# Attention values by halves of the queries, with the masked correction cut to 64 keys and its high and low part stacked

## The chip, the cores and the metric

The kernel runs on one core of one Trainium2 chip. The metric is the device time of one execution in microseconds (us). Five engines work side by side, each through its own instructions in the order in which they are written: TensorE (PE; PEld is its weight loading), VectorE (DVE), ScalarE (ACT), GpSimd (POOL) and SyncE (SP), which issues most of the DMA transfers. POOL and ACT issue some transfers too.

## The reference, cut to what matters

One residual block of a decoder, sequence 1024, width 1024, in float32. The part that is changed is sliding-window attention: 16 heads of 64, in four groups that share keys and values, blocks of 128 queries, a window of 128 keys, and one learned sink per head.

```
s = jnp.einsum('bnqkgd,bnskd->bnkgqs', qb, kb) * (1.0 / math.sqrt(hd))
diff = qi + BLOCK - kj
band = (diff >= 0) & (diff < WINDOW)
...
p = jnp.exp(s - m)
denom = jnp.sum(p, axis=-1, keepdims=True) + jnp.exp(sink - m)
o = jnp.einsum('bnkgqs,bnskd->bnqkgd', p / denom, vb)
```

A query q of a block (0 to 127) sees the keys 0 to q of its own block and the keys q+1 to 127 of the block before: for each key position exactly one of the two blocks. So there are 128 weights for a query, and the output is the sum over k of p[k] times v of the previous block, plus, where k is at most q, p[k] times the difference of the two v. The other parts of the block (input projection, rotary embedding, a gated linear recurrence, gates, the output projections, two norms) are unchanged. The first block of a sequence has no previous one.

## The kernel before

Matmuls work on float32 numbers that are split into a high and a low part, and the large projections use a scheme with seven half-size products for eight. Everything runs in an order that is written out by hand (`manual_schedule` for all five engines): instructions reach each engine in program order. In the input projection, a slot holds one product of twelve 128x512 matmuls, and `background` places further groups of ACT and DVE steps by planned costs; `slots(d)` waits d slots.

**Preparation of v.** `v_prep(g)` runs for each of the four groups g of heads in that background: `f0` loads v of the group, `f1` takes the difference d of neighbouring blocks (for the first block v itself), `f2` writes the high parts of v and d into the tiles `vs` and `dv` (columns 0 to 63), `f3` the low parts (columns 64 to 127), and stores both tiles to `vs_d[g]` and `dv_d[g]` from SP, 512 KB each. The tiles have one buffer each, so `f2` of the next group writes over what those stores read.

**Attention.** There are 32 units u: group u // 8, block n = u % 8. Four heads are handled at once, so a unit's weights are a tile of 128 keys x (4 heads x 128 queries). One pass of the loop is called a step here and works on several units, in this program order:

- `scores(u)`: eight matmuls into `s_ps`; `maxima_a` (ACT copy of the current block's scores to `p`), `maxima_d` (DVE lays the previous block's scores over them where the key is past the query, L1297; for n = 0 POOL fills with -1e30 instead, L1300; then the maximum, L1302). The units of one pair share a load of keys and queries (`load_kq`, SP).
- `weights_a(u-1)`: four exponentials on ACT (L1307).
- `piece()`: twelve matmuls of the recurrent branch's output projection (L174; the last products of the input projection, L696, in the first steps), whose weights ACT casts (L104) and DVE splits (L110).
- `weights_d(u-1)`: reciprocal and normalization on DVE (L1313, L1314).
- `values(u-3)`: the products of this case (L1355) into `pv`. Then `join_a` (ACT, L1364 and L1365) and `join_d` (DVE, L1375 and L1376) add the high and low halves of the output rows.
- `transposed(u-2)`: four transposes into `pt` (L1321); `split_a` casts the high part `phc` (ACT, L1326), `split_d` subtracts the low part `plc` (DVE, L1332).
- POOL: `sink(u+1)` copies the sinks (L1271); `masks(u-2)` makes `phm` and `plm`, copies of `phc` and `plc` with zeros where the key is past the query (L1341).
- DVE and ACT: the output gate of a finished pair (`a_prep`: L1491, L1496, L1501), one of its steps in each pass, and `do_later`: L104 and L110 for the coming pieces.

`values` multiplies the full pieces by `vs` of the previous block and the masked pieces by `dv`: four matmuls with 512 columns. For n = 0 there are two, with `dv`. `load_v(m)` brings `vs` and `dv` of a pair of units from HBM through POOL's queue, two transfers, and stands inside `values` of the even units. `phc`, `plc`, `phm`, `plm`, `pt`, `pv` and `s_ps` have one buffer each.

Of the kernel before, what the change touches and what calls it, by code (L numbers as in the profile page):

```python
# [12 lines left out]
F32 = mybir.dt.float32  # L13
F32R = mybir.dt.float32r
# [4 lines left out]
ALU = mybir.AluOpType  # L19
# [3 lines left out]
P = 128  # L23
# [5 lines left out]
NG = 4  # L29
# [23 lines left out]
def tile_hybrid_block(ctx, tc, x, x_t, pk, rows, posr, posi, c_row, w_ss, w_gate, w_main, w_v,  # L53
                      w_g, w_ap, w_rp, w_out, out):
    nc = tc.nc
    V, A, G, T = nc.vector, nc.scalar, nc.gpsimd, nc.tensor

    def dma(dst, src, eng=nc.sync):
        dst, src = (a.bitcast(F32) if a.dtype == F32R else a for a in (dst, src))
        return eng.dma_start(dst, src)  # L60

    def f32(ap):
        return ap.bitcast(F32)
# [65 lines left out]
    vs_d = [tc.dram_tile([P, 8, P], F32, name=f"vs_d{g}") for g in range(NG)]  # L129
    dv_d = [tc.dram_tile([P, 8, P], F32, name=f"dv_d{g}") for g in range(NG)]  # L130
# [440 lines left out]
    def make_operands(i):  # L571
        for t in (i, i + 4):
# [8 lines left out]
    W = {}  # L581
# [11 lines left out]
                    channel_multiplier=-1)  # L593
# [47 lines left out]
    class Load:  # L641

        pe = act = dve = 0.0
# [555 lines left out]
    def v_prep(g):  # L1199
        t = {}  # L1200
        vpp = W["vpp"]

        def f0():
            t["v"] = vpp.tile([P, 8, 64], F32, tag="v32", name="v32")
            dma(t["v"][:], v_d[:, :, g, :])

        def f1():
            t["d"] = vpp.tile([P, 8, 64], F32, tag="d32", name="d32")
            V.tensor_tensor(out=t["d"][:, 1:8, :], in0=t["v"][:, 1:8, :],
                            in1=t["v"][:, 0:7, :], op=ALU.subtract)  # L1210
            V.tensor_copy(t["d"][:, 0, :], t["v"][:, 0, :])

        def f2():
            for n_ in ("vs", "dv"):
                t[n_] = vpp.tile([P, 8, P], F32R, tag=n_, name=n_)
            A.copy(t["vs"][:, :, 0:64], t["v"][:])
            A.copy(t["dv"][:, :, 0:64], t["d"][:])

        def f3():
            for n_, d_, dst in (("v", "vs", vs_d), ("d", "dv", dv_d)):  # L1220
                V.tensor_tensor(out=t[d_][:, :, 64:128], in0=t[n_][:],
                                in1=f32(t[d_][:, :, 0:64]), op=ALU.subtract)
# [8 lines left out]
    at = psx = None  # L1231
    U = {}
# [22 lines left out]
        dma(qs[:], q_d[g].rearrange("(a j) t -> a j t", j=4)[:, :, t0:t0 + 256])  # L1255
        U["kq", m] = ks, qs

    def load_v(m):
        g, n0 = m // 4, (m % 4) * 2
        vs = at.tile([P, 2, P], F32R, tag="vs", name="vs", bufs=2)  # L1260
        dv = at.tile([P, 2, P], F32R, tag="dv", name="dv", bufs=2)
        dma(dv[:], dv_d[g][:, n0:n0 + 2, :], G)
        lo = 0 if n0 else 1
        dma(vs[:, lo:, :], vs_d[g][:, n0 - 1 + lo:n0 + 1, :], G)
        U["v", m] = vs, dv

    def sink(u):
        px = at.tile([P, 4, P + 1], F32, tag="p", name="p", bufs=3)
# [64 lines left out]
        U["m", u] = phc, plc  # L1333

    def masks(u):
        phc, plc = U["m", u]
        ms = []
        if u % 8:
            for s_, tag in ((phc, "phm"), (plc, "plm")):
                d_ = at.tile([P, 4, P], F32R, tag=tag, name=tag)  # L1340
                G.affine_select(out=d_[:], in_=f32(s_[:]), pattern=[[0, 4], [1, P]],  # L1341
                                compare_op=ALU.is_ge, fill=0.0, base=0,
                                channel_multiplier=-1)
                ms.append(d_)
        U["m", u] = [phc, plc], ms

    def values(u):
        n = u % 8
        vs, dv = U["v", u // 2]
        full, masked = U.pop(("m", u))  # L1350
        prods = [((vs if n else dv)[:, n % 2, :], m) for m in full]
        prods += [(dv[:, n % 2, :], m) for m in masked]
        pv = psx.tile([P, 4 * P], F32, tag="v", name="pv")
        for i, (b, m) in enumerate(prods):
            W["pe"] = T.matmul(pv[:], b, m[:].rearrange("p j q -> p (j q)"),  # L1355
                               start=(i == 0), stop=(i == len(prods) - 1))
        U["pv", u] = [pv[:].rearrange("p (a e q) -> p a e q", a=2, e=2)]
# [280 lines left out]
    for u in range(32 + 3):  # L1638
# [178 lines left out]
    for c in range(2, KC):  # L1817
# [21 lines left out]
        if c > 5:  # L1839
            n = 0 if c == 6 else 3  # L1840
# [84 lines left out]
    for n in range(24):  # L1925
        p, kc = n // 4, n % 4
# [67 lines left out]
    for i in range(3):  # L1994
        f = fs[i]
# [8 lines left out]
    f = small()  # L2004
# [91 lines left out]
```

## Time and profile before

| | |
|---|---|
| median of 3 runs | 912.93 us (912.89 to 913.12) |
| profiled execution, span from first to last instruction | 910.2 us |
| the runs' median less that span (start and end around it) | 2.7 us |
| PE busy | 892.0 us, 98% of the span |
| DVE busy | 722.1 us, 79% |
| ACT busy | 557.6 us, 61% |
| POOL busy | 125.2 us, 14% |
| moved by DMA | 182.05 MB, 200 GB/s over the span |
| attention, first scores to last values | 563 to 735 us |

The page gives no own time for the profiled execution beside its span; the runs' times are those of whole executions. A line of the timeline has the start in us from the span's start, the duration in us, the engine, the line of the kernel, the operation, the tiles as written<-read, shapes, and in brackets the engine's idle time before it and who ended it. The groups give count, busy time, mean duration in ns and idle time before. Matmuls are pipelined, so their recorded durations overlap.

### The profile page before, as it was taken

What the parts mean: (1) busy time and instruction counts of PE and PEld (TensorE: products, weight loads), DVE (VectorE), ACT (ScalarE), POOL (GpSimd) and SP (SyncE); (2) the same over time, 40 slices, a digit from 0 to 9 for tenths busy, and PEclk for the clock granted to TensorE, in tenths of its full rate; (3) what the DMA queues carried; (4) which work ended last, traced back from release to release, by engine and by line L of the source; (5) the groups of instructions that cost most, each with busy time, mean ns of one, the idle gap of its engine ahead of it and who ended that gap; (6) DMA issues with size and microseconds to landing.
All of it is one profiled execution on the core that took longest, in us unless ns stands there. A gap on an engine that the chain in (4) does not pass through costs nothing.

```text
span 910.2 us, 12609 instructions
## 1 busy us (share of the span) xinstructions
PE 892.0 (98%) x4187; PEld 740.7 (81%) x4187; DVE 722.1 (79%) x1143; ACT 557.6 (61%) x1088; POOL 125.2 (14%) x204
## 2 busy tenths in 40 slices
PE   5999999999999999999999999999999999999997
PEld 3879888887888788888887888888888888888886
DVE  7976889797679983988498576899999946779875
ACT  6753655454566755775678685888888731114555
POOL 0120000000010010000000001354444421310002
PEclk9999999999999999999999999999999999999998
DMA  9963458862344362346155257996666259878314
GB/s 351 414 212 110 163 168 312 281 230 85 116 144 151 116 234 86 115 151 225 36 197 166 84 192 253 338 368 215 203 199 219 93 172 330 306 273 322 140 46 185
DMA packets 88598, 182.05 MB, mean 200 GB/s; under 512 B 13891, under 2 KB 30275, under 8 KB 88534
## 3 DMA queue, kind: packets, MB, share of 16 engines
q1 hardware_dynamic: 81908, 161.57, 51.0%
q0 software_dynamic: 6336, 19.37, 5.9%
q8 instruction: 33, 0.54, 0.2%
q14 instruction: 31, 0.25, 0.1%
q10 hardware_dynamic: 290, 0.32, 0.1%
HBM read 124.49 MB, written 57.12 MB: 200 GB/s over the span
## 4 chain that ended last, share of the span: by engine, by line
PE 87%; DVE 5%; DMA 4%; ACT 2%; issue 1%; POOL 0%; SPq 0%; DVEq 0%; ACTq 0%
PE bk L696 43%; PE rp L174 13%; PE bo L1869 7%; PE pmain L174 6%; PE pgate L991 5%; PE bk L174 3%; PE s_ps L1283 3%; PE pv L1355 2%; DMA r<-w_main 2%; PE pt L1321 1%; DVE wl L110 1%; PE bk L1529 1%; PE bk L1528 1%; PE bk L1527 1%; DMA wada<-w_ss 1%
## 5 line engine op out<-in xcount | busy, mean ns | idle before, releaser
L696 PE MATMUL bk<-nh,wl 128*128 128x512 f32 x352 | 137.4, 390 | 0.4 <-DVE wl L110 0.4
L696 PE MATMUL bk<-nh,wh 128*128 128x512 f32 x352 | 137.1, 389 | 0.0
L696 PE MATMUL bk<-nl,wh 128*128 128x512 f32 x352 | 137.0, 389 | 0.0
L110 DVE TENSOR_TENSOR wl<-r,wh 128x512 fp32r<-128x512 f32 x113 | 80.5, 727 | 7.4 <-ACT wh L104 7.4
L104 ACT CAST wh<-r 128x512 fp32r<-128x512 f32 x113 | 68.6, 618 | 21.6 <-PE bk L1529 12.2
L60 POOL DMA_DIRECT2D wq_d<-wq x32 | 22.0, 687 | 423.7 <-DVE wq L1181 379.3
L696 PEld LDWEIGHTS bk<-nh,wl 128*128 128x128 f32 x352 | 66.1, 188 | 15.1 <-DVE wl L110 1.5
L696 PEld LDWEIGHTS bk<-nh,wh 128*128 128x128 f32 x352 | 66.1, 188 | 13.8
L696 PEld LDWEIGHTS bk<-nl,wh 128*128 128x128 f32 x352 | 66.1, 188 | 13.6
L696 PE MATMUL bk<-hh,wl 128*128 128x512 f32 x176 | 68.6, 390 | 0.4 <-DVE wl L110 0.4
L696 PE MATMUL bk<-hh,wh 128*128 128x512 f32 x176 | 68.6, 390 | 0.0
L696 PE MATMUL bk<-hl,wh 128*128 128x512 f32 x176 | 68.5, 389 | 0.0
L110 DVE TENSOR_TENSOR wl<-ws,wh 128x512 fp32r<-128x512 f32 x76 | 51.7, 683 | 0.0
L1307 ACT ACTIVATE p<-p,small 128x129 f32<-128x129 f32 x128 | 50.1, 401 | 0.0
L104 ACT CAST wh<-ws 128x512 fp32r<-128x512 f32 x76 | 45.8, 614 | 0.1
L1869 PE MATMUL bo<-wh,sum 128*128 128x512 f32 x128 | 39.6, 389 | 0.0
L696 PEld LDWEIGHTS bk<-hh,wh 128*128 128x128 f32 x176 | 33.0, 188 | 7.7 <-ACT wh L104 0.9
L696 PEld LDWEIGHTS bk<-hh,wl 128*128 128x128 f32 x176 | 33.0, 188 | 7.5 <-DVE wl L110 0.8
L696 PEld LDWEIGHTS bk<-hl,wh 128*128 128x128 f32 x176 | 33.0, 188 | 6.9
L1283 PE MATMUL s_ps<-ks,qs 128*128 128x256 f32 (+1 forms) x256 | 37.6, 289 | 0.2 <-DVE p L1297 0.2
L799 ACT ACTIVATE c<-bk 128x512 f32<-128x512 f32 x29 | 17.3, 597 | 30.2 <-PE bk L696 30.2
L696 PE MATMUL bk<-hha,wl 128*128 128x512 f32 x88 | 34.5, 392 | 0.6 <-DVE wl L110 0.5
(412 smaller groups left out, 2336.7 us busy)
## 6 DMA issues: line engine op xcount, KB each, us to landing
r<-w_main SPq DMA_DIRECT2D x100, 256.0 KB, 4.3
wada<-w_ss SPq DMA_DIRECT2D x16, 512.5 KB, 9.0
qs<-q_d SPq DMA_DIRECT2D x16, 512.0 KB, 5.8
wq_d<-wq POOLq DMA_DIRECT2D x24, 256.0 KB, 4.6
wr<-wq_d SPq DMA_DIRECT2D x24, 256.0 KB, 5.0
ks<-k_d SPq DMA_DIRECT2D x24, 192.0 KB, 5.0
wq<-w_out POOLq DMA_DIRECT2D x16, 256.0 KB, 5.7
q_d<-rhi SPq DMA_DIRECT2D x16, 256.0 KB, 4.1
```

Of the source, the lines that this page charges most:

```text
L60: return eng.dma_start(dst, src)
L104: A.copy(dst[0][:], src)
L110: V.tensor_tensor(out=dst[1][:], in0=src, in1=f32(dst[0][:]), op=ALU.subtract)
L174: mm = T.matmul(ps[hf], ww, xx[kc][hf], start=(kc == 0 and ww is w_h and xx is xh), stop=(kc == KC - 1 and xx is xl))
L696: W["pe"] = T.matmul(ps, ww[:, c], b[kc][xx_], start=(first and kc == 0 and i == 0), stop=(kc == 3 and i == 2), skip_group_check=not first)
L799: A.activation(t["t"], s(), AF.Tanh, scale=0.5)
L991: W["pe"] = T.matmul(ps[:, SL[hf]], ww[:, c0:c0 + P], xx_[:, SL[hf]], start=(ic == 0 and i == 0), stop=(ic == 1 and i == 2))
L1283: W["pe"] = T.matmul(o, qs[:, j, qc], ks[:, b, k0 + (0 if n else P):k0 + 256], start=(b == 0), stop=(b == 1))
L1307: A.activation(px[:, j, :], px[:, j, :], AF.Exp, bias=sm[:, 0, j:j + 1], accum_out=sm[:, 1, j:j + 1])
L1321: W["pe"] = T.transpose(pt[:, j, :], px[:, j, 0:P], ident[:])
L1355: W["pe"] = T.matmul(pv[:], b, m[:].rearrange("p j q -> p (j q)"), start=(i == 0), stop=(i == len(prods) - 1))
L1869: T.matmul(bank[p][i] if dst is None else dst, a[:, ts_], b[:][:, sl], start=(new and kc == 0 and j == 0), stop=(kc == 3 and j == 2), skip ...
```

## The change

- `v_prep`: `f3` no longer stores `vs` and `dv` as they are. It writes, for each block, four tiles of 128 keys x 128 columns to one array `vx_d[g]`: the full v for the first half of the queries (all 128 keys from the previous block), the full v for the second half (keys 0 to 63 from the own block, 64 to 127 from the previous one), and for each half of the queries the difference `dv` of its 64 keys, twice, one below the other. That takes nine transfers for a group, all issued from POOL.
- `load_v(u)` loads the four tiles of one unit (256 KB) in one transfer from POOL's queue, three buffers deep. It is called in every pass, after `masks(u-2)`.
- `masks(u)` makes two tiles `pm0` and `pm1`, one for each half of the queries: the 64 keys of that half, the high part in partitions 0 to 63 and the low part in 64 to 127, times 4 heads x 64 queries. That takes four selects on POOL with 64 partitions x 256 elements, where there were two with 128 x 512.
- `values(u)` takes, for each half of the queries, the two full pieces (the 256 columns of that half) and the stacked masked piece: six matmuls with 256 columns, where there were four with 512. For the first block of a group it takes two with 512 columns, as before.

```diff
         def f3():
-            for n_, d_, dst in (("v", "vs", vs_d), ("d", "dv", dv_d)):
+            lo, hi, x_ = slice(0, 64), slice(64, 128), vx_d[g]
+            for n_, d_ in (("v", "vs"), ("d", "dv")):
                 V.tensor_tensor(out=t[d_][:, :, 64:128], in0=t[n_][:],
                                 in1=f32(t[d_][:, :, 0:64]), op=ALU.subtract)
-                dma(dst[g], t[d_][:])
+            vs, dv = t["vs"], t["dv"]
+            dma(x_[:, 1:8, 0, :], vs[:, 0:7, :], G)
+            dma(x_[:, 0, 0, :], vs[:, 0, :], G)
+            dma(x_[lo, :, 1, :], vs[lo], G)
+            dma(x_[hi, 1:8, 1, :], vs[hi, 0:7, :], G)
+            dma(x_[hi, 0, 1, :], vs[hi, 0, :], G)
+            for i, half in enumerate((lo, hi)):
+                for rows_ in (lo, hi):
+                    dma(x_[rows_, :, 2 + i, :], dv[half], G)
...
+    def load_v(u):
+        vx = at.tile([P, 4, P], F32R, tag="vx", name="vx", bufs=3)
+        dma(vx[:], vx_d[u // 8][:, u % 8, :, :], G)
+        U["v", u] = vx
...
     def masks(u):
-        phc, plc = U["m", u]
+        pieces = U["m", u]
         ms = []
         if u % 8:
-            for s_, tag in ((phc, "phm"), (plc, "plm")):
-                d_ = at.tile([P, 4, P], F32R, tag=tag, name=tag)
-                G.affine_select(out=d_[:], in_=f32(s_[:]), pattern=[[0, 4], [1, P]],
-                                compare_op=ALU.is_ge, fill=0.0, base=0,
-                                channel_multiplier=-1)
+            for h in range(2):
+                c = slice(64 * h, 64 * h + 64)
+                d_ = at.tile([P, 4, 64], F32R, tag=f"pm{h}", name=f"pm{h}")
+                for i, s_ in enumerate(pieces):
+                    G.affine_select(out=d_[64 * i:64 * i + 64], in_=f32(s_[c, :, c]),
+                                    pattern=[[0, 4], [1, 64]], compare_op=ALU.is_ge, fill=0.0,
+                                    base=0, channel_multiplier=-1)
                 ms.append(d_)
...
     def values(u):
...
+        vx = U.pop(("v", u))
+        pieces, masked = U.pop(("m", u))
+        pv = psx.tile([P, 4, P], F32, tag="v", name="pv")
+        for h in range(2 if masked else 1):
+            c = slice(64 * h, 64 * h + 64) if masked else slice(0, P)
+            prods = [(h, m[:, :, c]) for m in pieces]
+            if masked:
+                prods.append((2 + h, masked[h][:]))
+            for i, (b, m) in enumerate(prods):
+                W["pe"] = T.matmul(pv[:, :, c], vx[:, b, :], m, start=(i == 0),
+                                   stop=(i == len(prods) - 1))
...
-        if n % 2 == 0 and u // 2 + 1 < 16:
-            load_v(u // 2 + 1)
...
             masks(u - 2)
+        if 1 <= u < 32:
+            load_v(u)
```

More of the change, by code (lines that the diff above doesn't have):

```diff
@@ L128, in tile_hybrid_block @@
     v_d = tc.dram_tile([P, 8, NG, 64], F32, name="v_d")
-    vs_d = [tc.dram_tile([P, 8, P], F32, name=f"vs_d{g}") for g in range(NG)]
-    dv_d = [tc.dram_tile([P, 8, P], F32, name=f"dv_d{g}") for g in range(NG)]
+    vx_d = [tc.dram_tile([P, 8, 4, P], F32, name=f"vx_d{g}") for g in range(NG)]
     gate_d = tc.dram_tile([1, D], F32, name="gate_d")
@@ L1256, in load_kq @@
         U["kq", m] = ks, qs
[L1258 to L1265, printed above, removed]
+    def load_v(u):
+        vx = at.tile([P, 4, P], F32R, tag="vx", name="vx", bufs=3)
+        dma(vx[:], vx_d[u // 8][:, u % 8, :, :], G)
+        U["v", u] = vx
     def sink(u):
@@ L1335, in masks @@
     def masks(u):
-        phc, plc = U["m", u]
+        pieces = U["m", u]
         ms = []
         if u % 8:
-            for s_, tag in ((phc, "phm"), (plc, "plm")):
-                d_ = at.tile([P, 4, P], F32R, tag=tag, name=tag)
-                G.affine_select(out=d_[:], in_=f32(s_[:]), pattern=[[0, 4], [1, P]],
-                                compare_op=ALU.is_ge, fill=0.0, base=0,
-                                channel_multiplier=-1)
+            for h in range(2):
[5 more added lines that the diff above has]
+                                    base=0, channel_multiplier=-1)
                 ms.append(d_)
-        U["m", u] = [phc, plc], ms
+        U["m", u] = pieces, ms
     def values(u):
[L1348 to L1357, printed above, removed]
-        if n % 2 == 0 and u // 2 + 1 < 16:
-            load_v(u // 2 + 1)
+        vx = U.pop(("v", u))
[9 more added lines that the diff above has]
+                                   stop=(i == len(prods) - 1))
+        U["pv", u] = [pv[:].rearrange("p (a e) q -> p a e q", a=2)]
     def join_a(u):
```

## The prediction

> **What bounds the kernel now.** I read the page first (busy shares, then the chain that ended last), then the chain as a list over the attention stage, then the stage's windows, then single steps of it.
>
> ```profile
> span 910.2 us, 12609 instructions
> PE 892.0 (98%) x4187; PEld 740.7 (81%) x4187; DVE 722.1 (79%) x1143; ACT 557.6 (61%) x1088; POOL 125.2 (14%) x204
> PE 87%; DVE 5%; DMA 4%; ACT 2%; issue 1%; POOL 0%; SPq 0%; DVEq 0%; ACTq 0%
> ...
> 669.92 0.95 PE s_ps L1283 x8
> 670.87 2.75 PE rp L174 x12
> 673.62 0.92 PE pv L1355 x4
> 674.53 0.44 PE pt L1321 x4
> ...
> 600.00:650.00 50.00, 49.82 (x278) 42.63 (x276) 47.33 (x86) 41.09 (x133) 25.37 (x40) 1.00 0.77 251
> 650.00:700.00 50.00, 50.00 (x282) 43.15 (x281) 45.73 (x85) 41.24 (x134) 22.07 (x38) 1.00 0.61 197
> ```
>
> The chain says PE, and the list shows the rhythm of one attention step: scores, 12 products of the recurrent projection, values, transposes: 0.95 + 2.75 + 0.92 + 0.44 = 5.05 us. In the windows (columns PE, PEld, DVE, ACT, POOL, granted clock, DMA share) PE has no idle time and a clock of 1.00, DVE is at 91 to 95%, ACT at 82%. So a shorter product shortens the step, as long as DVE, ACT and POOL hand over their part in time. How much time they have is the question of this case.
>
> **Term 1, the products.** A matmul's recorded 389 ns overlaps its neighbours; what a product costs is the distance from start to start.
>
> ```profile
> 673.46 0.39 PE L1355 MATMUL pv<-phc,vs 128*128 128x512 f32 x1
> ...
> 674.14 0.40 PE L1355 MATMUL pv<-plm,dv 128*128 128x512 f32 x1
> ...
> 69.97 0.28 PE L1527 MATMUL bk<-wh,hh 128*128 128x256 f32 x1
> ...
> 70.21 0.28 PE L1529 MATMUL bk<-wh,hl 128*128 128x256 f32 x1
> ```
>
> 512 columns: (674.14 - 673.46)/3 = 0.227 us. 256 columns with a fresh weight load each time (the v product, the same kind): (70.21 - 69.97)/2 = 0.120 us, a little over half. Before: four products, 4 x 0.227 = 0.908. After: two halves of three, 6 x 0.120 = 0.72. That is 0.188 us for each of the 28 units with a previous block: **-5.3 us** if all of it shows; the four first units of a group keep their two products. The new operands are read and written in runs of 64 columns; no row shows that, and the nearest row (runs of 256) has 0.120, which I take. From below, 0.11 is about half of 0.227 (-6.9 us in all); from above I allow 0.14 (-1.9).
>
> The Trainium skill ("TensorE: Matmul & The Clock Gate", Back-to-back issue gap) gives N/2.4 + 2.5 ns for a lone stream, so 216 and 109 ns, by which the term would be 28 x (0.863 - 0.655) = -5.8 us as an estimate. The trace has 227 and 120, so its own number decides.
>
> **Term 2, when the masks are ready.** Before, two selects on POOL mask the whole high and low pieces; after, four selects of 64 partitions x 256 fill the two stacked pieces: high half 0, low half 0, high half 1, low half 1. Only the first can run before the low piece exists; three come behind it, where one came before. What a select costs and meets:
>
> ```profile
> L592 POOL TENSOR_SCALAR_AFFINE_SELECT mf<-mf 128x128 f32<-128x128 f32 x1 | 0.3, 296 | 0.1
> ...
> 671.26 0.69 DVE L1332 TENSOR_TENSOR plc<-pt,phc 128x512 fp32r<-128x512 f32 x1
> 671.87 0.68 DVE L1491 TENSOR_TENSOR yq<-yq,r 128x512 f32<-128x512 f32 x1
> 672.03 1.02 POOL L1341 TENSOR_SCALAR_AFFINE_SELECT plm<-plc 128x512 fp32r<-128x512 f32 x1 [0.40 <-DVE plc L1332]
> 672.47 0.75 DVE L1297 COPY_PREDICATED p<-mgt,s_ps 128x512 f32<-128x512 uint32 x1
> ...
> 676.05 0.64 POOL L1341 TENSOR_SCALAR_AFFINE_SELECT phm<-phc 128x512 fp32r<-128x512 f32 x1 [0.82 <-ACT phc L1326]
> 676.29 0.69 DVE L1332 TENSOR_TENSOR plc<-pt,phc 128x512 fp32r<-128x512 f32 x1
> 676.90 0.68 DVE L1501 TENSOR_TENSOR al<-yq,ah 128x512 fp32r<-128x512 f32 x1
> 677.05 1.02 POOL L1341 TENSOR_SCALAR_AFFINE_SELECT plm<-plc 128x512 fp32r<-128x512 f32 x1 [0.36 <-DVE plc L1332]
> 677.50 1.12 DVE L110 TENSOR_TENSOR wl<-r,wh 128x512 fp32r<-128x512 f32 x1
> ...
> 679.18 0.39 PE L1355 MATMUL pv<-plm,dv 128*128 128x512 f32 x1
> ```
>
> A select over 512 columns takes 0.64 undisturbed and one over 128 takes 0.296, so 256 columns take about 0.41 by the line between them; that half the partitions makes it cheaper no row shows (ends: 0.30 and 0.50). The select of plc takes 1.02, because a DVE operation with two SBUF inputs (L1491, L1501) is already running: POOL ends 0.50 behind it instead of 0.64 after its own start. And it works the other way: L110 behind it takes 1.12 where such an operation takes 0.68. The two take turns. DVE operations that read PSUM (L1332, L1297) do not take part.
>
> Counted from the end of plc, the one select of before ends at 1.10 (673.05 - 671.95). After: the first of three ends at about 0.88 (1.10 less 0.22 for the half width). If DVE follows with L1297, the other two need 2 x 0.37 more: 1.6, which is **0.5 later**. If DVE follows with L110, that takes its turn until about 1.42, the second select ends at 1.70, the third at 2.1: **1.0 later**. Meanwhile PE comes 0.19 earlier in each cycle. So the last product waits unless the room between the end of the old select and the old last product was at least 0.71, or 1.20 with L110.
>
> The room: 674.14 - 673.05 = 1.09 in the first step above, 679.18 - 678.07 = 1.11 in the second. I read all 28 pairs this way; the first and the last, and the worst but one:
>
> ```profile
> 581.58 0.64 POOL L1341 TENSOR_SCALAR_AFFINE_SELECT plm<-plc 128x512 fp32r<-128x512 f32 x1
> 583.58 0.39 PE L1355 MATMUL pv<-plm,dv 128*128 128x512 f32 x1
> ...
> 722.38 1.02 POOL L1341 TENSOR_SCALAR_AFFINE_SELECT plm<-plc 128x512 fp32r<-128x512 f32 x1 [0.80 <-DVE plc L1332]
> 723.45 0.51 PE L1355 MATMUL pv<-plm,dv 128*128 128x512 f32 x1
> ...
> 733.28 1.02 POOL L1341 TENSOR_SCALAR_AFFINE_SELECT plm<-plc 128x512 fp32r<-128x512 f32 x1 [0.37 <-DVE plc L1332]
> 734.47 0.40 PE L1355 MATMUL pv<-plm,dv 128*128 128x512 f32 x1
> ```
>
> In 11 units L110 is the next turn of DVE; their rooms are 0.76, 0.22, 0.67, 1.11, 0.75, 0.73, 1.10, 0.73, 0.76, 0.05, 0.17, together 7.05, so the waits are 11 x 1.20 - 7.05 = 6.15 us. Of the 17 others nine have 1.03 or more and wait for nothing; the eight short ones (0.51, 0.05, 0.35, 0.34, 0.64, 0.39, 0.62, 0.42) wait 8 x 0.71 - 3.32 = 2.36. Five of these eight directly follow a unit that now waits; there ACT and DVE were behind and catch up during that wait, so I drop their 1.1. Sum: **+7.4 us**. With selects of 0.30 three of them end 0.33 sooner and the sum falls to about 3.4; with 0.50 it grows by 0.27 for each waiting unit to some 12.
>
> The stage's DVE and POOL work hardly changes: four selects of 0.41 against two of 0.64, one load issue for a unit against two for a pair of units, both behind the masks instead of ahead of the next sink copy, with nothing queued behind them but that copy. The loads (256 KB a unit, twice the bytes) are issued two steps, some 10 us, ahead; their buffer was freed by products that precede the transposes on PE. Zero.
>
> **Term 3, the preparation of v.** Eight stores leave SP (a small relief, counted as nothing) and 36 go to POOL, which is idle there. They are cut into runs of 512 bytes, 4096 for a group.
>
> ```profile
> L60 POOL DMA_DIRECT2D wq<-w_out x16 | 11.7, 733 | 10.5 <-DMA wq_d<-wq 10.5
> L60 POOL DMA_DIRECT2D dv<-dv_d x16 | 8.9, 555 | 0.5 <-DMA ks<-k_d 0.4
> dv_d<-dv SPq DMA_DIRECT2D x4, 512.0 KB, 4.6
> 139.85 0.68 DVE L1221 TENSOR_TENSOR dv<-d,dv 128x512 fp32r<-128x512 f32 x1
> 154.20 0.62 ACT L1216 CAST vs<-v 128x512 fp32r<-128x512 f32 x1
> 135.00:155.00 20.00, 20.00 (x90) 16.58 (x89) 18.68 (x32) 12.77 (x25) 0.00 (x0) 1.00 0.84 291
> ```
>
> 256 runs cost 0.733 us of POOL and 128 cost 0.555: 1.4 ns a run and 0.38 for each DMA, so 9 x 0.38 + 4096 x 0.0014 = 9.1 us a group, landing about 4.6 later. The next group's ACT copy overwrites the source tile 13.7 us after the subtraction: it fits just so, in a stretch where the DMA engines are 84% busy. If it is late, ACT waits, and what is queued behind it are the casts of the next weights; ACT is idle 36% of that window and PE not at all. I take 0, with an upper end of +2.
>
> **Sum.** -5.3 + 7.4 + 0 = +2.1 us, on 910.2. The runs' median of 912.93 lies 2.7 above that span, for what is around it; I leave that as it is: **915.0 us**.
>
> **Rivals.** *The masks are in time* (other side). If a select over half the partitions takes 0.25 or less, or three short ones slip between DVE's turns, the last ends no later than before; only the rooms under 0.19 wait (0.05, 0.05, 0.17, together 0.3) and the time is 912.9 - 5.0 = 907.9. Against it: nothing in the rows ties a select's cost to partitions. It decides from about 0.35 us a select, where gain and waits are equal. 18%.
>
> *The selects run side by side.* Two neighbours write different partitions (0-63, 64-127). If they overlap, the lateness is 0.19 in place of 0.5 and 0.7 in place of 1.0; the same sum over the rooms gives 3.4, so 912.9 - 1.9 = 911.0. The Trainium skill states the mechanism ("GPSIMD Engine Reference", Instruction dispatch): each core serves its own 16 partitions and starts the next instruction when its share is done. No pair of selects in this trace has disjoint partitions, so no run here shows it. 15%.
>
> *POOL becomes the pace.*
>
> ```profile
> 682.44 1.02 POOL L1341 TENSOR_SCALAR_AFFINE_SELECT plm<-plc 128x512 fp32r<-128x512 f32 x1 [0.72 <-DVE plc L1332]
> 683.42 1.08 POOL L1300 TENSOR_SCALAR_AFFINE_SELECT p<-p 128x512 f32<-128x512 f32 x1
> 684.53 0.69 DVE L1302 TENSOR_REDUCE small<-p 128x4 f32<-128x516 f32 x1 [0.53 <-POOL p L1300]
> ```
>
> At three of the group starts the fill of the first unit (L1300) stands behind the masks, and DVE's reduce already waits 0.53 for it. A fill 1.0 later delays all of DVE's queue, so the next unit's low piece, by as much: +3 us, and with a select of 0.45 another 2: 918 to 920. 25%.
>
> **How the numbers follow.** My case has 42%, with its own range 912.4 to 917.5. A measurement here tells about 0.2% (1.8 us). Faster by more: 18 + 7 of the side-by-side case + 2 = 27%. Within it: 8 + 17 of mine = 25%. Slower: 23 of mine + 25 = 48%. The range of 908.5 to 919 leaves out the tip of the fastest and of the slowest case.
>
> **What would show it.** Right: start to start 0.120 among the six products; selects of 0.4, the one behind plc about 0.8; PE's weight loads waiting for POOL in L1355 some 7 us in all where it was 1.0; steps without L110 at 4.86 us. Wrong: selects of 0.25 or overlapping in time, products at 0.14, or ACT waiting for the stores of v around 150 to 200 us.

## The result, and the profile after

The changed kernel takes 919.02 us (median of 4, 918.27 to 919.73) against 913.02 us (912.89 to 913.51) in the same job: a ratio of 1.0067, 95% interval 1.0053 to 1.0080. It is slower by 0.7%. The profiled execution took 919.73 us with a span of 917.8 (the other three: 916.3 to 917.5), 7.6 us over the span of before; these 7.6 are what the trace has to explain, the medians differ by 6.0. Two executions among the experiments took 4009 and 3531 us (one with unread masks, one with the fill on DVE); they are left out of the medians and ranges below.

The page of the changed kernel, its span, busy shares and the shares of the chain that ended last:

```profile
span 917.8 us, 12866 instructions
PE 892.6 (97%) x4243; PEld 742.6 (81%) x4243; DVE 720.0 (78%) x1143; ACT 556.6 (61%) x1088; POOL 163.0 (18%) x296
PE 79%; DVE 8%; ACT 4%; DMA 3%; issue 3%; POOL 3%; SPq 0%; ACTq 0%; DVEq 0%; POOLq 0%
```

PE's share of the chain fell from 87% to 79%, and POOL, which had no place in it, has 3%. The windows of the stage (columns as in the prediction):

```profile
600.00:650.00 50.00, 48.11 (x287) 42.00 (x286) 43.71 (x81) 40.19 (x129) 26.53 (x54) 1.00 0.83 274
650.00:700.00 50.00, 48.13 (x290) 42.00 (x289) 44.25 (x83) 39.36 (x129) 27.55 (x57) 1.00 0.68 219
```

PE stood idle 1.9 us in each 50 where it had been idle 0.2 and 0.0. DVE became less busy too (43.7 instead of 47.3): nothing is full, the engines wait for each other. The list of waits says for whom (us in total, times, longest); the last two rows are the same waits in before:

```profile
PEld pv L1363 <- POOL pm L1347: 10.8, 19, 1.3
DVE small L1306 <- POOL p L1304: 10.6, 4, 5.2
PE pv L1363 <- POOL pm L1347: 6.8, 15, 1.1
```
```profile
PEld pv L1355 <- POOL plm L1341: 1.0, 2, 0.6
DVE small L1302 <- POOL p L1300: 6.5, 3, 5.4
```

The weight loads of the masked products wait for POOL 19 times. (PEld's and PE's figures overlap. Start to start of the value products, less 0.120 for each, gives 12.5 us in all; the same reading of before, less 0.227, gives 0.8.) DVE's reduce waits for the fill on POOL; the longest of these waits, 5.2 and 5.4, stands at the start of the stage, the others at the later group starts. One unit shows both causes. It is unit 14, counted from 0, ahead of a group start; the timeline of POOL, DVE and PE:

```profile
645.71 0.41 POOL L1347 TENSOR_SCALAR_AFFINE_SELECT pm<-plc 64x256 fp32r<-64x256 f32 x1
...
646.07 0.55 POOL L60 DMA_DIRECT2D vx<-vx_d  x1
...
646.68 0.63 POOL L1304 TENSOR_SCALAR_AFFINE_SELECT p<-p 128x512 f32<-128x512 f32 x1
...
647.34 0.69 DVE L1306 TENSOR_REDUCE small<-p 128x4 f32<-128x516 f32 x1 [1.98 <-POOL p L1304]
...
649.83 0.69 DVE L1336 TENSOR_TENSOR plc<-pt,phc 128x512 fp32r<-128x512 f32 x1
...
650.53 0.28 PE L1363 MATMUL pv<-phc,vx 128*128 128x256 f32 x1
...
650.64 0.32 PE L1363 MATMUL pv<-plc,vx 128*128 128x256 f32 x1
650.65 0.74 POOL L1347 TENSOR_SCALAR_AFFINE_SELECT pm<-plc 64x256 fp32r<-64x256 f32 x1 [2.16 <-DVE plc L1336]
...
651.46 0.41 POOL L1347 TENSOR_SCALAR_AFFINE_SELECT pm<-phc 64x256 fp32r<-64x256 f32 x1
...
651.93 0.41 POOL L1347 TENSOR_SCALAR_AFFINE_SELECT pm<-plc 64x256 fp32r<-64x256 f32 x1
...
652.40 0.19 PEld L1363 LDWEIGHTS pv<-pm,vx 128*128 128x128 f32 x1 [0.54 <-POOL pm L1347]
```

Read it from the bottom. The last product waits for the third select behind plc, which ends at 652.34, 1.82 us after plc did. The selects follow each other at 0.47, where one takes 0.41. The low piece itself was late: it ended at 650.52, when the first value product started; in an ordinary unit it is 1.5 us ahead. And it was late since DVE's queue had stood 1.98 us at the reduce of the group start, behind the fill on POOL; in before this wait was 0.53. The fill queues behind two things: the previous unit's four selects, and the issue of the load of v that now follows them in every pass and takes 0.55 us of POOL. In before the fill came right behind the select (683.42, in the prediction's last view).

What the selects cost, over the whole stage (duration in ns, min/median/max):

```profile
L1347 POOL TENSOR_SCALAR_AFFINE_SELECT pm<-phc x56: 405/412/857, 580.3 to 740.6; 64x256 fp32r<-64x256 f32 x56
L1347 POOL TENSOR_SCALAR_AFFINE_SELECT pm<-plc x56: 408/500/843, 581.4 to 741.4; 64x256 fp32r<-64x256 f32 x56
```

For all kernels below I use three lengths: **ahead**, from the span's start to the first matmul of the scores; **stage**, from there to the last matmul of the values; **tail**, the rest of the span. The rows for before (whose last matmul, at 734.47, stands in the prediction) and for after:

```profile
563.10 0.44 PE L1283 MATMUL s_ps<-ks,qs 128*128 128x128 f32 x3
```
```profile
563.02 0.44 PE L1287 MATMUL s_ps<-ks,qs 128*128 128x128 f32 x3
...
741.91 0.39 PE L1363 MATMUL pv<-pm,vx 128*128 128x256 f32 x1 [0.67 <-POOL pm L1347]
```

So before is 563.1 + 171.4 + 175.7 and after 563.0 + 178.9 + 175.9: all of the loss, 7.5 us, lies in the stage. The products as reckoned, -5.3, and the new waits, +11.7, come to 6.4 of it; the scores' wait for DVE's copy, 0.4 in before, is gone, which leaves 6.0. The rest is the clock behind the two longest of these waits, at unit 29 (columns as in the prediction):

```profile
726.00:730.00 4.00, 2.41 (x14) 1.82 (x13) 2.38 (x5) 2.73 (x12) 2.90 (x4) 0.95 0.61 204
730.00:734.00 4.00, 4.00 (x13) 3.15 (x12) 2.30 (x5) 0.47 (x1) 1.83 (x4) 0.63 0.18 58
```

At a clock of 0.63 for 4 us PE loses 4 x 0.37 = 1.5 us of work, and a little at 0.95 ahead of that. Read from start to start, the products of the recurrent branch take 84.43 us in the stage where they took 82.86: 1.6 more. With it the sum is 7.6 where 7.5 are seen.

### The profile page after: what moved, and what is told of

It is laid out like the page before. It is cut to its first block, busy times and chain, and to the rows that moved or that the text cites. A ratio compares the mean times of both kernels' runs of the same rounds, so it can differ in the third digit from the quotient of the medians.

```text
span 917.8 us, 12866 instructions
## 1 busy us (share of the span) xinstructions
PE 892.6 (97%) x4243; PEld 742.6 (81%) x4243; DVE 720.0 (78%) x1143; ACT 556.6 (61%) x1088; POOL 163.0 (18%) x296
## 4 chain that ended last, share of the span: by engine, by line
PE 79%; DVE 8%; ACT 4%; DMA 3%; issue 3%; POOL 3%; SPq 0%; ACTq 0%; DVEq 0%; POOLq 0%
PE bk L695 42%; PE rp L173 9%; PE bo L1877 7%; PE pmain L173 6%; PE pgate L990 5%; PE bk L173 3%; POOL pm L1347 2%; PE s_ps L1287 2%; PE pv L1363 1%; DVE plc L1336 1%; DVE wl L110 1%; PE bk L1535 1%; PE bk L1534 1%; PE bk L1533 1%; DMA r<-w_main 1%
## 5 line engine op out<-in xcount | busy, mean ns | idle before, releaser
L110 DVE TENSOR_TENSOR wl<-r,wh 128x512 fp32r<-128x512 f32 x113 | 78.1, 705 | 7.5 <-ACT wh L104 7.5
L60 POOL DMA_DIRECT2D wq_d<-wq x32 | 21.9, 686 | 278.3 <-DVE wq L1180 234.0
L110 DVE TENSOR_TENSOR wl<-ws,wh 128x512 fp32r<-128x512 f32 x76 | 51.6, 681 | 0.0
L1347 POOL TENSOR_SCALAR_AFFINE_SELECT pm<-plc 64x256 fp32r<-64x256 f32 x56 | 32.3, 577 | 26.4 <-DVE plc L1336 24.6
```

Source lines behind the costliest of these rows:

```text
L110: V.tensor_tensor(out=dst[1][:], in0=src, in1=f32(dst[0][:]), op=ALU.subtract)
L1347: G.affine_select(out=d_[64 * i:64 * i + 64], in_=f32(s_[c, :, c]), pattern=[[0, 4], [1, 64]], compare_op=ALU.is_ge, fill=0.0, base=0, cha ...
```

## The experiments

The letters in the expectations are the theories as each states them. Where not otherwise said, the edit is to the changed kernel, and ahead, stage and tail are of the profiled execution; the ratios stand against runs of the kernel before in the same job.

**1. What the products alone are worth.** The first run drops the selects (the masked correction is left out; the third product reads the low piece), the second makes the selects and doesn't read them (the same part is left out).

```diff
-    prods.append((2 + h, masked[h][:]))
+    prods.append((2 + h, pieces[1][:, :, c]))
```

> The changed kernel with the four selects left out; the third product of each half reads columns of the low piece instead of a masked piece, so the masked correction is left out of the result. Theory A (the shorter products save what was forecast, and all of the loss is PE waiting for late masks): nothing is waited for, so -5.3 us and the 1.1 us of waits that the kernel before had: 906.5 to 908. Theory B (products on runs of 64 columns, the doubled loads or the 36 stores on POOL cost time of their own): 911 or more.

> The changed kernel with the four selects made as before, but read by nobody; the third product of each half reads columns of the low piece, so the masked correction is left out of the result. POOL's and DVE's work, their turns and the fill behind the masks stay. Theory A (the waits for masks): 907 to 909, no wait of L1363 for POOL. Theory C (the more numerous turns of POOL slow DVE, and that sets the pace): 915 or more, as DVE's operations are as late as in the changed kernel.

Without selects: 912.49 us (906.09 to 915.57, 10 runs), ratio 0.9985 (0.9966 to 1.0005); with unread ones 911.45 (910.12 to 914.68, 9 runs), ratio 0.9994 (0.9982 to 1.0006). Without selects the fastest run is in theory A's range and the median in theory B's, and the spread of 9.5 us was in neither. With unread ones the median is over theory A's 909 and under theory C's 915. The trace of the first: ahead 563.3, stage 172.5, tail 175.5. Its waits, and the windows behind them:

```profile
PE s_ps L1287 <- DMA qs<-q_d: 4.2, 2, 3.7
```
```profile
618.00:622.00 4.00, 1.23 (x8) 0.82 (x6) 3.19 (x7) 3.94 (x14) 0.73 (x2) 0.96 1.04 368
622.00:630.00 8.00, 7.07 (x27) 6.12 (x28) 4.55 (x8) 3.20 (x12) 0.00 (x0) 0.59 0.91 258
```

Nothing waits for masks any more. A load of q is late instead (the DMA engines are at a share of 1.04), the clock falls to 0.59 behind the wait, and the two together cost 6.3 us. The second run has the other loss: ahead 567.6. Its stage is 169.7, some 4 us over the 165.7 below: even where nobody reads the selects, the scores wait for DVE's copy and the value products for the late low piece (2.2 and 1.8 us of PEld), the latter at units 6, 14 and 22 for the most part. Both are the subject of points 4 and 5. A later run of the first kernel, with another queue for the stores of v, had the load in time, and gives the price of the products:

```diff
-            dma(x_[:, 1:8, 0, :], vs[:, 0:7, :], G)
+            dma(x_[:, 1:8, 0, :], vs[:, 0:7, :])        # and so the other eight
```

> The version without selects (the masked correction is left out, the third product reads the low piece) with the nine stores on SP. It is the price of the products alone. Theory T plus late loads (in the no-select run profiled, TensorE waited 3.7 us at 619 us for the DMA qs<-q_d and then ran at a clock of 0.66 for 10 us, 6.3 us in all): executions at 906.5 to 908 where the load is in time, up to 913 where it isn't; median 907 to 910. If the products' gain of 5.3 us does not exist: 912 or more in all executions.

914.57 us (909.13 to 918.27, 12 runs), ratio 1.0017 (1.0001 to 1.0034): its median is over the 907 to 910 of theory T, and one execution of the twelve is under the 912 of the other case. In the trace ahead grew to 569.5 (point 4). The stage is 165.7, which is 5.7 us under before. From start to start the value products take 21.9 us there and 27.9 in before, 0.8 of which were waits: the products gave 5.1 to 5.3 of the 5.3 that were reckoned.

**2. The lateness of the masks, made without the new products.** The kernel before, with its two selects cut into four of 128x256 in the changed kernel's order:

```diff
-    for s_, tag in ((phc, "phm"), (plc, "plm")):  # one select of 512 columns each
+    for h in (slice(0, 2), slice(2, 4)):          # high, low, high, low
+        for d_, s_ in zip(ms, (phc, plc)):        # 256 columns each
```

> The kernel before with its two selects cut into four of 128 partitions x 256, in the order high, low, high, low; the four products with 512 columns, the loads and the stores of v as before. Theory A: three selects come behind the low piece, the last 1.83 us after its end (2.16 where L110 takes a turn) in place of 1.10, so 0.73 or 1.06 later than before; against the rooms that were read these are waits of some 7 us, and up to 3 more by the fill behind them: 918 to 922. If only the new shape of the products or of the loads is to blame: 913. A select of 128 x 256 takes 0.41, as one of 64 x 256 does, if partitions do not matter; about 0.8 or so if they do.

917.63 us (916.49 to 918.31), ratio 1.0051 (1.0037 to 1.0066); stage 176.0, so the four selects and their order alone cost 4.6 us; the time is just under the 918 to 922 expected. The waits, the duration of a select, and the reduce behind the fill at the group start of unit 16:

```profile
PEld pv L1355 <- POOL phm L1342: 5.6, 12, 1.3
PEld pv L1355 <- POOL plm L1342: 3.0, 15, 0.6
```
```profile
L1342 POOL TENSOR_SCALAR_AFFINE_SELECT plm<-plc x56: 403/528/857, 581.7 to 739.0; 128x256 fp32r<-128x256 f32 x56
```
```profile
646.78 0.69 DVE L1302 TENSOR_REDUCE small<-p 128x4 f32<-128x516 f32 x1 [1.25 <-POOL p L1300]
```

Over 128 partitions a select takes no longer (403 ns at the least) than over 64 (408). The reduce waits 1.25 us here, where no issue of a load stands between selects and fill, 0.53 in before and 1.98 in the changed kernel. So of the 1.45 us by which the change lengthened that wait, the four selects make 0.72, and the other 0.73 is the load's issue in POOL's queue, by difference.

**3. Taking parts of the lateness away.** First the order of the selects, then the place of the join (ACT's and DVE's addition of the two halves of the values, which stands ahead of the split of the next unit and itself waits for the late product), then both; and the second alone in the kernel before.

```diff
-    for h in range(2):                    # high 0, low 0, high 1, low 1
-        for i, s_ in enumerate(pieces):
+    for i, s_ in enumerate(pieces):       # high 0, high 1, low 0, low 1
+        for h in range(2):
```
```diff
             values(u - 3)
-            join_a(u - 3)
-            join_d(u - 3)
...
             split_d(u - 2)
+        if u >= 3:
+            join_a(u - 3)
+            join_d(u - 3)
```

> The changed kernel with the same four selects in the order high half 0, high half 1, low half 0, low half 1. Two in place of three come behind the low piece. Theory A: the last ends about 1.35 us behind it (1.68 with a turn of L110), 0.25 or 0.58 later than the one select of before; with the 0.19 that PE gains the waits are 2.7 us by the rooms and about 1 for the fill: 910 to 912, faster than before. Theory C (POOL's amount of work or number of turns): as the changed kernel, 918 to 920.

> The changed kernel with join_a and join_d of unit u-3 after transposed, split_a and split_d of unit u-2 in the loop, on ACT and DVE. The high piece comes right behind the transposes instead of behind two ACT copies, so the low piece and the masks come about 0.77 us earlier against PE. Theory A: waits only where the room was under 0.17 (under 0.48 with a turn of L110), some 1.1 us, and 0 to 1.5 for the fills: 908 to 910.5. Theory C (number of turns, DVE's amount of work): 917 or more.

> The changed kernel with both: join behind split, and the selects in the order high, high, low, low. Theory A: no unit waits but perhaps the last ones, the whole 5.3 us shows and the 1.1 us of waits of before go too: 906.8 to 908.5. This is the version that should beat both kernels.

> The kernel before with join_a and join_d behind transposed, split_a and split_d, nothing else. It tells how much of the last two is the reordering alone. Theory A: PE sets the pace and only its 1.1 us of waits can go: 911.8 to 913. If the order of the join is worth something by itself: under 911.

Low selects last: 913.52 us (911.68 to 919.2, 12 runs), ratio 1.0015 (1.0000 to 1.0029), stage 171.2. Join behind the split: 914.94, ratio 1.0027 (1.0013 to 1.0041), stage 173.6. Both: 912.55 (909.91 to 920.32, 12 runs), ratio 1.0004 (0.9986 to 1.0021), stage 169.3. Before with the join moved: 913.24 (911.8 to 913 expected), ratio 1.0006 (0.9997 to 1.0015), stage 172.5. The waits for masks, of low selects last and of both:

```profile
PEld pv L1362 <- POOL pm L1347: 4.2, 8, 0.7
```
```profile
PEld s_ps L1287 <- DVE p L1301: 2.3, 7, 0.7
...
PEld pv L1362 <- POOL pm L1347: 0.2, 1, 0.2
```

With both orders the value products wait 0.2 us for masks, and the stage is 2.1 us shorter than that of before. Each of the two edits alone saves 7.7 and 5.3 us of stage, both together 9.6; that is less than the sum, as two edits to the same chain would give. Some of the join's gain is taken back by DVE (the 2.3 us of the first row: its copy out of the scores' PSUM tile comes later, and the next scores wait for the tile), which is also why it costs the kernel before 1.1 us of stage. The times of the three versions of the changed kernel are over their expectations by 1.5, 4.4 and 4.1 us, and the version with both is no better than before: its profiled execution lost 1.5 us ahead and 1.0 in the tail, and the join's version about 2 us in the stage to loads that came late (yl, yh and q, 0.5 to 1.2 us each).

**The fill at the group starts.** DVE makes it in the place of POOL:

```diff
-    G.affine_select(out=p, in_=p, ..., fill=-1e30, base=0, channel_multiplier=1)
+    V.copy_predicated(p, mgt, neg)       # neg: a tile of -1e30, both spread over 4 heads
```

> The changed kernel with the fill of the first unit of a group made on DVE (a predicated copy of a constant) instead of on POOL (L1304). Theory A with the fill as the part that the forecast had too small: DVE no longer waits behind the masks at the group starts, the units 6, 14 and 22 lose their waits of 1.2 to 1.7 us for the most part, against 0.7 us of DVE for each fill: 915 to 917. If the fill is of no account: 919.

916.16 us (915.57 to 916.86), ratio 1.0038 (1.0023 to 1.0054), within the 915 to 917 expected. It ran once more, for its trace:

> The changed kernel with the fill of the own keys' scores made by DVE (a predicated copy from a tile of -1e30) in the place of POOL, once more, for its trace. Theory P (the fill that queues behind the selects at the group starts is the 3.1 us by which units 6, 14 and 22 wait more than reckoned): their waits for masks fall from 1.70, 1.38 and 1.18 us to 0.7 or less each, the whole of the waits from 12.5 to 9 to 10 us, time 915.5 to 917. Rival (the selects alone are late there, whoever fills): these three keep 1.2 us or more, and what is saved lies elsewhere.

917.15 us (915.76 to 917.93), just over the 917 expected, ratio 1.0042 (1.0027 to 1.0056), stage 176.3, 2.6 us under the changed kernel's. Unit 14 there, and the total of the weight loads' waits:

```profile
644.40 0.94 DVE L1306 COPY_PREDICATED p<-mgt,neg 128x512 f32<-128x512 uint32 x1
...
645.44 0.69 DVE L1308 TENSOR_REDUCE small<-p 128x4 f32<-128x516 f32 x1
...
647.78 0.69 DVE L1338 TENSOR_TENSOR plc<-pt,phc 128x512 fp32r<-128x512 f32 x1
...
649.99 0.28 PE L1365 MATMUL pv<-phc,vx 128*128 128x256 f32 x1
...
650.58 0.29 PE L1365 MATMUL pv<-pm,vx 128*128 128x256 f32 x1
```
```profile
PEld pv L1365 <- POOL pm L1349: 8.5, 14, 1.3
```

The reduce follows the fill at once, the low piece ends 1.5 us ahead of the values (648.47 against 649.99), and six products take 0.59 from the first start to the last: no wait. By start to start, units 6, 14 and 22 wait 0.99, 0 and 0 us where they had 1.70, 1.38 and 1.18; unit 6 so keeps more than the 0.7 expected, which is the 0.98 that the prediction had for it. Units 13 and 21, where DVE's copy now meets the selects, wait 0.7 us more between them. All value products together wait 9.9 us, within the 9 to 10 expected.

**4. The preparation of v.** Theory N had it covered, as the prediction did. The kernel before with the nine stores of a group on POOL (and the three loads a pair of units that read the new array):

```diff
-    dma(dst[g], t[d_][:])                  # two a group, on SP
+    dma(x_[:, 1:8, 0, :], vs[:, 0:7, :], G)  # nine a group, on POOL, as in the changed kernel
```

> The kernel before with one thing of the change: the nine stores of a group of v on POOL in the place of SP's two (the loads of v read the new array in 3 transfers a pair of units; selects and products as before). Theory T (the preparation costs something in many executions): ACT's copy into the second group's dv waits until the last store of the first group but one has landed; in the executions seen it landed at 175.7 to 180.0 us, and TensorE lost 0, 0.35, 1.7 and 4.6 us at about 180 us; so a median 1 to 4 us over before (913.7 to 917) with a spread of 3 us or more, and a wait of ACT dv for the DMA vx_d<-dv in the profile. Theory N (the preparation is covered, as the prediction's third term had it, and the spread of the other runs is of another cause): 912.3 to 913.4, spread under 1.5.

914.41 us (912.86 to 916.06, 11 runs), ratio 1.0014 (1.0005 to 1.0023): theory T's median and spread. ACT does wait at the third group of v:

```profile
177.64 0.62 ACT L1216 CAST dv<-d 128x512 fp32r<-128x512 f32 x1 [4.47 <-DMA vx_d<-dv]
```

(The expectation named the first and second group; it is the third group's copy that waits for the second group's stores.) But TensorE hardly felt it in this execution: ahead is 563.6, 0.5 over before. Of the 3.1 us of span over before, 1.2 are in the stage and 1.5 in the tail, where TensorE waits at 808 us behind transfers of wq, long after the stores of v. So the wait is shown here, and its price is not. It has a price in two other traces: with unread selects and with both orders ahead is 4.5 and 1.5 us longer, and the chain there runs through the last store of the second group, the copy it holds up, and the weights behind that copy.

The nine stores on SP instead, in the changed kernel:

> The changed kernel with the nine stores of v on SP in the place of POOL; all else as changed. Theory T: the stores that land late are gone, if SP's land earlier: 916.5 to 918.5, spread under 1.5, the stage from the first score on as in the changed kernel (12.5 us of waits of the value products). Theory N: 918.0 to 919.7, as changed. If SP's queue becomes the late one (it carries the weight loads too), over 920.

925.42 us, ratio 1.0132 (1.0119 to 1.0145); ahead 569.2, stage 179.3 as changed. It is the third case of the expectation. What else SP issues stands behind them: ACT waits for other stores, and at 215 to 217 us TensorE waits for a load of weights, which SP issued only behind the nine stores of the fourth group (199.0 to 205.7) and others. The wait, and the chain:

```profile
ACT rhi L625 <- DMA q_d<-rhi: 12.4, 3, 6.1
```
```profile
210.38 5.23 DMA r<-w_main
...
217.53 6.97 PE bk L695 x23
```

The stores themselves landed sooner than from POOL (us from issue to landing, median; first the changed kernel, then this one):

```profile
vx_d<-dv POOLq DMA_DIRECT2D x16, 256.0 KB, 8.3
vx_d<-dv SPq DMA_DIRECT2D x16, 256.0 KB, 4.1
```

The DMA engines were at a share of 0.98 from 160 to 180 us in both, so a full stretch alone doesn't make the landing late. The late landing goes with POOL's queue; what in that queue does it, these runs don't show.

The version with both orders and SP's stores was no better:

> The changed kernel with the two selects of the high piece first, the join behind the split, and the nine stores on SP. Theory T: the version with both orders had 912.6 median and 909.9 at the lowest; without the late stores 908.5 to 911, which is faster than before by 0.2 to 0.4%. Theory N: 912 to 913 as with the stores on POOL.

918.23 us (915.86 to 924.96), ratio 1.0066 (1.0043 to 1.0088). The profiled execution is the slowest of the seven: ahead 570.7, stage 175.1 with a load of q that came 3.4 us late.

Then one group of v was put later, by the planner's own slots, on the kernel before with nine stores and on the version with both orders:

```diff
-    [("S", 0, 0, f0)], slots(4), [("D", 0, 0.85, f1)],
+    [("S", 0, 0, f0)], slots(7 if g == 1 else 4), [("D", 0, 0.85, f1)],
```

> The kernel before with the nine stores on POOL, as in the run of 914.41, and the second group of v put three planner slots (about 8 us) later. Theory T (ACT's copy into dv comes before the last store of the first group has landed): the wait of ACT dv for the DMA is gone or under 0.5 us in the profile, TensorE loses nothing at 160 to 220 us, median 912.7 to 913.5. Theory D (the doubled traffic delays other transfers, wherever the copy stands): 914 to 915 as before, with waits elsewhere.

> The version with both orders (high selects first, join behind the split) and the second group of v three slots later. Theory T: 910.0 to 911.7 median against 912.55 with the group at its place, so faster than before by 0.15 to 0.3%. Theory D: 912 to 913.5, with waits of TensorE for late loads (qs, yl, w_out) from 560 us on.

918.25 us, ratio 1.0052 (1.0037 to 1.0066), and 916.67, ratio 1.0035 (1.0022 to 1.0049): both worse than any theory had it, ahead 568.5 and 568.0. The chain of the first of them in order of time, and its wait, say why:

```profile
172.21 10.59 DMA vx_d<-dv
...
183.03 0.63 ACT dv L1216
```
```profile
ACT dv L1216 <- DMA vx_d<-dv: 4.6, 1, 4.6
```

I had moved the second group, whose stores are waited for, and not the third, whose copy waits. For a move of the third by three slots there is no time. With the third moved by two slots:

```diff
+    [("S", 0, 0, f0)], slots(6 if g == 2 else 4), [("D", 0, 0.85, f1)],
```

> The kernel before with the nine stores on POOL and the third group of v two planner slots later (ACT's copies of that group two operations and some 3 us later; the other groups at their places). In the run with the second group later the stores that are waited for had moved, not the copy that waits: the second group's last store landed at 182.8 us, the third group's copy into dv waited 4.6 us for it, and TensorE lost 5.4 us. Theory T: now the copy comes 3 us nearer to the landing (175.7 to 180.0 us seen), ACT's wait for the DMA vx_d<-dv is under 1.5 us, TensorE loses under 0.5 us at 160 to 220 us, median 912.7 to 913.7. Theory D (the doubled traffic costs wherever the copy stands): 914 to 915.

> The version with both orders (high selects first, join behind the split) and the third group of v two slots later. Theory T: the loss of 0 to 4.6 us at 180 us is gone in most executions: median 910.0 to 911.7, faster than before by 0.15 to 0.35%, lowest 908 to 910. Theory D: 912 to 913.5.

The kernel before with nine stores: 913.53 us (912.33 to 914.32, 11 runs), ratio 1.0004 (0.9994 to 1.0014), ahead 563.1, no wait of ACT for those stores in the trace. So the wait goes when the copy comes 3 us later with the same traffic, as theory T had it, and the time can't be told from before. That the lower median comes from this wait isn't shown: the two ratios' intervals overlap, and the profiled execution with the copy at its place had lost only 0.5 us ahead.

**5. Where the gain of the best version went.** With both orders and the third group later the loss ahead is gone (563.0), but the time is 913.03 us (909.85 to 917.12, 12 runs), ratio 1.0004 (0.9989 to 1.0020); the stage is 172.6 in place of 169.3. The waits there, and the window:

```profile
PE s_ps L1287 <- DMA qs<-q_d: 2.7, 1, 2.7
```
```profile
610.00:620.00 10.00, 9.70 (x56) 8.35 (x56) 9.47 (x19) 7.90 (x27) 2.90 (x8) 1.00 1.06 333
620.00:630.00 10.00, 6.77 (x41) 5.85 (x42) 7.07 (x13) 5.77 (x17) 3.40 (x9) 1.00 0.95 283
```

It is the load of q again, at the same unit as in the run without selects: up to 620 us the DMA engines have no room. The changed kernel's trace has no such wait: its PE comes to each unit later. Theory D, by which the doubled traffic costs wherever the copy stands, so finds waits for loads in this stage; whether the doubled loads of v make q late or only the earlier demand does, these runs don't separate. Loading q earlier, into more buffers, wasn't tried. No version here is faster than before beyond what the runs can tell.

## Why the prediction was wrong

It said 915.0 us, slower, with a range of 908.5 to 919; the time is 919.02. The direction and the main mechanism, products that wait for POOL's selects, were right. The step that failed is the sum of term 2 over the units: it gave 7.4 us of waits on top of those of before, and 11.7 were measured. It counted each unit's masks from its own low piece and took that piece at its old place; at three group starts the fill on POOL makes the piece late.

- **Term 1**, six products at 0.120: right. Six products take 0.59 us from the first start to the last where nothing waits (650.58 - 649.99), so 0.118 each, and without selects the products gave 5.1 to 5.3 us. The Trainium skill's 109 ns for a lone stream ("TensorE: Matmul & The Clock Gate", Back-to-back issue gap) are not reached.
- **Term 2**, the price of a select: right, 0.41 expected and 0.405 to 0.412 measured, and independent of the partitions, as was taken. So the rival in which the masks are in time is out. The three behind plc were put at 0.88, then 0.37 for each other; they come 0.47 apart, and the last ends 1.82 behind plc instead of 1.6 (2.16 with L110, 2.1 expected).
- **Term 2**, the sum over the units: too small by 4.3. By unit, 3.1 of it are units 6, 14 and 22 (reckoned 0.98, 0.07 and 0.09, of which the last two fall under those dropped behind a unit that waits; measured 1.70, 1.38 and 1.18). With the fill on DVE the waits of 14 and 22 are gone and unit 6 has 0.99, close to what was reckoned, so the fill on POOL is the cause. Another 0.6 is unit 29, whose last select meets a second turn of DVE, and 0.6 units 3 to 5.
- **The fill's delay** has a part that was put at nothing: the prediction let the issue of the load stand behind the masks "with nothing queued behind them but that copy", and at the group starts the fill is queued there too. By the run with four selects in before that is 0.73 of the 1.45 us. The fill itself was foreseen, but as a rival (POOL becomes the pace, 918 to 920, 25%), when it is certain as soon as what stands in front of it ends later: it belonged in the sum. That rival's +3 us came out, with a fill that was 1.45 late and not 1.0, so its size is partly luck; and its 918 to 920 was reached with the help of the clock and unit 29, which it didn't have.
- **The rival of selects side by side** is out: neighbours that write different halves of the partitions start 0.47 apart where one takes 0.41, and never overlap. The Trainium skill ("GPSIMD Engine Reference", Instruction dispatch) has each core go on when its own share is done; these traces show no overlap from it.
- **Term 3**, the stores of v: 0 in the profiled execution of the changed kernel, but not covered. I put their landing at 4.6 us, the median of the old stores, which SP issued; from POOL the last store of the second group took 9 to 14 us in a stretch where the DMA engines are full, and the copy came just ahead or just behind. The chain of the version with unread selects has the longest:

```profile
166.38 13.60 DMA vx_d<-dv
```

  With the groups at their places the loss ahead was 0 to 4.5 us in the traces; the upper end of +2 was too little.
- **Not in the sum at all**: the lower clock behind a stall of PE, 1.6 us in the profiled execution. Two of the four executions had a mean clock of 0.996 and spans of 917.8 and 917.5, two had 0.998 and 916.6 and 916.3, so it may not be the same in all.

## What to carry to other kernels

Where a change makes work on a side engine longer, or puts a DMA issue into its queue, follow the whole queue and not only the product that waits: what stands behind is late as well, and through another engine it comes back a unit later, in the very input whose time was taken as given. A faster product earns nothing where a mask, a store or a load was only just in time; read the room of each of these before counting the gain. And a transfer's landing time is taken from the stretch and the queue it will run in, not from a median over another queue's in quieter ones.

## What the runs showed of the hardware

- TensorE's granted clock fell without a long pause: with single waits of at most 1.3 us and PE busy for 2.41 of 4.00 us, the next 4 us ran at 0.63. A wait of 3.7 us brought 0.59 over 8 us; but in the last version above one of 2.7 us left it at 1.00. The Trainium skill ("TensorE: Matmul & The Clock Gate", HAM oscillation) asks for no idle gap over some 3.4 us; in the first of these cases no gap is that long, and the clock fell all the same. How far the clock follows the waits alone stays open.
- A select on POOL over 256 columns costs 0.41 us over 64 partitions and over 128 alike, and one follows another at 0.47.
- The issue of a load from POOL holds up POOL's own work: the issue of a load of v took 0.55 us (646.07 to 646.62), and the fill behind it started at 646.68.
- Nine stores of a group of v from POOL took a median of 8.3 us to land (tiles from dv) and the last of the second group 9 to 14, where the two old stores from SP, of 512 KB each, had 4.6. From SP the same nine landed in 4.1, with the DMA engines as full (a share of 0.98 from 160 to 180 us in both), but the kernel was slower by 6 us, as SP's other transfers stood behind them.
